# Opening products 512 columns wide, one token tile at a time, and softmax transposes moved inside the values' pass, in a two-layer float32 decoder trunk

## The chip, the cores and the metric

The kernel runs on one core of a Trainium2 chip. The metric is the device time of one execution in microseconds (us); the median over runs of the same program is compared.

## The reference

256 tokens of width 2048 go through two layers in float32. Layer 0 mixes tokens by causal pooling, layer 1 by dilated attention with three head groups; each layer ends in an MLP with squared ReLU, and every residual sum is layer-normed:

```
def strided_window_attention(q, k, v, dil, n_back, slopes): ...
    s = einsum(q, k) / sqrt(E) - slope * distance        # masked to the window
    p = softmax(s);  o = p @ v                           # and its log-sum-exp

def dilated_attention(x, w_qkv, w_out):
    qkv = (x @ w_qkv).reshape(B, S, 3, 3, 8, 128)        # type, group, slot
    merged = sum over groups of softmax(lse) * o
    return merged @ w_out                                # 1024 -> 2048

def sqrelu_mlp(x, w_up, w_down):
    h = relu(x @ w_up)                                   # 2048 -> 8192
    return (h * h) @ w_down

def reference(x, ...):
    for i in range(2):
        h = pool_mixer(x, ...) if i == 0 else dilated_attention(x, ...)
        x = layer_norm(ALPHA * x + h)
        x = layer_norm(ALPHA * x + sqrelu_mlp(x, ...))
```

## The kernel before, in words

Every float32 product is made of three products of rounded halves: an operand is split into a high part (a copy to the type float32r, on ACT, line 62) and a low part (the difference, on DVE, line 63), and high by high, low by high and high by low are summed in PSUM. Weights are streamed from HBM once, in chunks of 128 x 1024 numbers (512 KB). A chunk goes through three steps: a DMA into one of four `raw` tiles (line 125, issued by SP as soon as a tile is free), the copy `wh` on ACT and the difference `wl` on DVE into one of eight pairs of split tiles (`prefetch`, line 129). `weights()` hands out the next pair and first asks for the eight that follow; `resident(n)` hands out n at once, which stay in use until the last product that reads them. A `raw` tile is free when `wl` is done, a split pair when PE has done the products that read it. The order of work on PE, ACT and DVE is the order in which the code is written; each of these engines goes through its own list in order.

There are two forms of product. In `feature_major` (line 186) the weights are the stationary operand and the moving one is `xT`, the transposed x: per 128 rows of the weights and 128 columns, one matmul of 512 and one of 256. In `token_products` (line 239) 128 tokens of x are stationary and the weights move, 256 or 512 columns at a time, for each of two token tiles t. PSUM has eight banks, one tag with eight buffers, given out in rotation: a bank is written again eight allocations later, and waits until its readers are done.

A mixer or an MLP ends in `closing` (line 374), where the last 256 columns are made for token tile 0 first and then for tile 1, so that the norm of tile 0 runs beside tile 1's products. The normed tokens are transposed by PE (`ptr`, line 321), scaled on ACT (`xv`, line 330) and split on DVE into `xT` (lines 336 and 337). What follows a norm begins with `opening` (line 436): it takes the first 256 columns of the next weights, which are four chunks, does tile 0's products with all of them while tile 1 is still being normed (`normalise`, line 315), puts tile 1's transposes in, and then does tile 1's products with the same chunks. Line 447 asks for two more chunks before tile 1's products are issued. The norm's gain and bias are put on x itself later, in four `restore` steps (lines 352 and 353 on DVE, each two tiles of two operations), which `drain()` takes one at a time.

There are three openings: before the first MLP, before the attention, before the second MLP. In an MLP the opening's 256 columns go through `hidden` (ReLU `r` and square `q` on ACT, lines 531 and 533), then 256 columns and three times 512 columns follow feature-major; the opening's squares are transposed by PE (line 551) after the first of these. In the attention the opening makes the values of group 0 of the first pair of slots (`sp` 0); the values of the other two groups come in two passes of 256 columns (`project_value`). For later `sp` one pass of 512 columns makes two groups' values (`project_values`), and the softmax transposes (`transposes`, line 680) of the first slot stand behind it, followed by `values` (line 688), whose results go to bank `po`.

## Time and profile before

| | |
|---|---|
| median of 3 runs | 2147.08 us (2146.9 to 2147.69) |
| profiled execution: its time | 2146.52 us |
| profiled execution: its span | 2144.7 us |
| granted TensorE clock over the span | 0.999 |
| PE busy | 2124.7 us, 99% of the span |
| DVE busy | 1283.4 us, 60% |
| ACT busy | 1052.8 us, 49% |
| HBM read | 400.61 MB, 188 GB/s over the span |
| chain that ended last | PE 96%, DVE 2%, DMA 1%, ACT 1% |

The span runs from the first to the last instruction that the profiler recorded; the time of the execution has 1.8 us around it. Matmuls are pipelined: one 512 columns wide is shown as busy for some 390 ns, while the next starts after less, so distances between starts tell the rate. In the rows L62 is line 62, an arrow in brackets names what ended an engine's idle time, and a row with xN joins N instructions in a run.

### The profile page before, as it was taken

The numbers are of one execution on the slowest core, as the hardware profiler recorded it, in microseconds if no ns is written. First come the engines' busy times: TensorE is split into PE (matmuls) and PEld (weight loads), VectorE is DVE, ScalarE is ACT, GpSimd is POOL, SyncE is SP. The second block draws the span as 40 slices with busy tenths as digits, with TensorE's granted clock in tenths as the row PEclk, the third lists the DMA queues.
The fourth block names the chain that finished last, engine by engine and source line by source line (L and its number), as shares of the span: only waits on it lengthen the run. The fifth ranks groups of instructions, "written<-read, shape, count | busy, mean of one in ns | idle before, by whom it ended". The sixth has DMA issues, their size and how long they took to land.

```text
span 2144.7 us, 29773 instructions
## 1 busy us (share of the span) xinstructions
PE 2124.7 (99%) x11745; PEld 1845.9 (86%) x11745; DVE 1283.4 (60%) x1558; ACT 1052.8 (49%) x1368; POOL 23.0 (1%) x52
## 2 busy tenths in 40 slices
PE   8999999999999999999999999999999999999998
PEld 7889888888888888898998988888888888888887
DVE  6785756555455555578656565676655555554555
ACT  4563655454355355354545444455545534644541
POOL 1000000000000000001000000000000000000000
PEclk9999999999999999999999999999999999999999
DMA  7565567556655655548555555456665566566562
GB/s 239 204 216 177 169 204 237 175 199 201 191 185 196 194 172 206 194 139 237 173 175 161 176 162 173 164 164 218 209 221 178 201 197 188 176 207 186 181 207 94
DMA packets 256045, 404.67 MB, mean 189 GB/s; under 512 B 13104, under 2 KB 109984, under 8 KB 255648
## 3 DMA queue, kind: packets, MB, share of 16 engines
q1 hardware_dynamic: 253472, 394.31, 56.7%
q0 software_dynamic: 2432, 8.45, 1.9%
q8 instruction: 92, 1.51, 0.3%
q14 instruction: 49, 0.40, 0.1%
HBM read 400.61 MB, written 2.10 MB: 188 GB/s over the span
## 4 chain that ended last, share of the span: by engine, by line
PE 96%; DVE 2%; DMA 1%; ACT 1%; issue 0%; SPq 0%; DVEq 0%; ACTq 0%
PE pt L245 45%; PE pf L202 32%; PE pf L204 16%; PE pf L221 1%; PE pq L658 1%; PE po L697 1%; DMA raw<-in_attn_w_qkv 0%; DVE wl L63 0%; PE ptr L321 0%; DMA xz<-in_x 0%; ACT xv L330 0%; DVE xT L337 0%; DVE vL L63 0%; PE ptr L458 0%; DVE xT L336 0%
## 5 line engine op out<-in xcount | busy, mean ns | idle before, releaser
L63 DVE TENSOR_TENSOR wl<-raw,wh 128x1024 fp32r<-128x1024 f32 x744 | 898.2, 1224 | 621.1 <-ACT wh L62 607.1
L62 ACT ACTIVATE wh<-raw 128x1024 fp32r<-128x1024 f32 x744 | 773.4, 1057 | 805.8 <-PE pt L245 351.4
L202 PE MATMUL pf<-xT,wh 128*128 128x512 f32 x3008 | 947.6, 396 | 0.0
L204 PEld LDWEIGHTS pf<-xT,wl 128*128 128x128 f32 x3008 | 566.0, 188 | 134.0 <-DVE wl L63 0.6
L204 PE MATMUL pf<-xT,wl 128*128 128x256 f32 x3008 | 592.2, 278 | 0.0
L202 PEld LDWEIGHTS pf<-xT,wh 128*128 128x128 f32 x3008 | 459.5, 189 | 0.5
L245 PE MATMUL pt<-wl,hH 128*128 128x512 f32 (+1 forms) x1088 | 407.0, 377 | 0.0
L245 PE MATMUL pt<-wh,hH 128*128 128x512 f32 (+1 forms) x1088 | 407.0, 377 | 0.0
L245 PE MATMUL pt<-wh,hL 128*128 128x512 f32 (+1 forms) x1088 | 398.2, 377 | 0.0
L245 PEld LDWEIGHTS pt<-wl,hH 128*128 128x128 f32 x1088 | 204.8, 188 | 37.6 <-DVE wl L63 0.4
L245 PEld LDWEIGHTS pt<-wh,hH 128*128 128x128 f32 x1088 | 204.8, 188 | 37.5
L245 PEld LDWEIGHTS pt<-wh,hL 128*128 128x128 f32 x1088 | 199.6, 188 | 37.1
L245 PE MATMUL pt<-wh,xT 128*128 128x256 f32 (+1 forms) x704 | 156.4, 314 | 1.9 <-DVE xT L336 1.5
L245 PEld LDWEIGHTS pt<-wh,xT 128*128 128x128 f32 x704 | 117.2, 191 | 10.6 <-DVE xT L336 3.1
L63 DVE TENSOR_TENSOR hL<-q,hH 128x512 fp32r<-128x512 f32 x62 | 42.9, 693 | 125.6 <-ACT hH L62 125.6
L245 PE MATMUL pt<-wl,xT 128*128 128x256 f32 (+1 forms) x352 | 106.7, 312 | 0.0
L230 ACT ACTIVATE low<-pf 128x256 f32<-128x256 f32 x188 | 61.3, 377 | 69.6 <-PE pf L204 62.7
L245 PE MATMUL pt<-wh,pT 128*128 128x512 f32 (+1 forms) x320 | 82.6, 347 | 0.0
L231 DVE TENSOR_TENSOR u<-pf,low 128x256 f32<-128x256 f32 x172 | 64.7, 418 | 26.0 <-ACT low L230 26.0
L245 PEld LDWEIGHTS pt<-wl,xT 128*128 128x128 f32 x352 | 67.2, 191 | 3.6
L531 ACT ACTIVATE r<-u 128x512 f32<-128x512 f32 x62 | 39.2, 632 | 51.0 <-DVE u L231 51.0
L245 PEld LDWEIGHTS pt<-wh,pT 128*128 128x128 f32 x320 | 56.1, 189 | 7.5
(126 smaller groups left out, 1001.8 us busy)
## 6 DMA issues: line engine op xcount, KB each, us to landing
raw<-in_mlp_w_up SPq DMA_DIRECT2D x256, 512.0 KB, 4.4
raw<-in_mlp_w_down SPq DMA_DIRECT2D x256, 512.0 KB, 4.5
raw<-in_attn_w_qkv SPq DMA_DIRECT2D x120, 512.0 KB, 4.3
raw<-in_pool_w_in SPq DMA_DIRECT2D x32, 512.0 KB, 5.4
raw<-in_pool_w_out SPq DMA_DIRECT2D x32, 512.0 KB, 4.7
raw<-in_attn_w_qkv SPq DMA_DIRECT2D x48, 256.0 KB, 3.3
raw<-in_attn_w_out SPq DMA_DIRECT2D x16, 512.0 KB, 4.4
raw<-in_pool_w_group SPq DMA_DIRECT2D x8, 512.0 KB, 5.0
```

The source lines that it names most:

```text
L62: nc.scalar.activation(hi, src, AF.Copy)
L63: nc.vector.tensor_sub(lo, src, hi.bitcast(F32))
L202: nc.tensor.matmul(ps[b], hi[:, j, sl], a, start=(k == 0), stop=False, skip_group_check=True)
L204: nc.tensor.matmul(ps[b][:, 0, :], lo[:, j, sl], a[:, 0, :], start=False, stop=(k == nk - 1), skip_group_check=True)
L221: nc.tensor.matmul(ps[b // 2][:, b % 2, :], w[:, j, sl], a[:, part, :], start=(k == 0 and i == 0 and b % 2 == 0), stop=(k == nk - 1 and i ...
L230: nc.scalar.activation(low, p[:, 1, :], AF.Copy)
L231: nc.vector.tensor_add(out[:, b, :], p[:, 0, :], low)
L245: nc.tensor.matmul(ps, a[:, sl], u, start=(start and k == 0 and i == 0), stop=(k == nk - 1 and i == 2), skip_group_check=True)
L531: nc.scalar.activation(r, ps, AF.Relu)
L658: nc.tensor.matmul(pq[:, t, :], q[u][:, b, sl], k[v][:, b, :], start=(i == 0), stop=(i == 2))
L697: nc.tensor.matmul(po, v[:, st, b * P:(b + 1) * P], p[:, g, sl], start=(i == 0), stop=(i == 3 * 2 * GROUPS - 1))
```

## The change

The openings take 512 columns, eight chunks, instead of 256. Each token tile gets a PSUM bank of its own (before, both shared one), and the two chunks asked for ahead of tile 1's products are no longer asked for there. In an MLP the 256 columns that followed are part of the opening, and its squares need eight transposes instead of four. In the attention the opening makes the values of groups 0 and 1 of `sp` 0; group 2's follow by `project(2)`. The first slot's softmax transposes stand ahead of the last chunk of the values' pass for `sp` above 0, and behind the next `project(0)` for `sp` 0.

```diff
-UP_FIRST = (256, 256, 512, 512, 512)
 UP_REST = (512, 512, 512, 512)
-QKV_FIRST = ((2, 0), (0, 0), (1, 0), (0, 1), (1, 1), (0, 2), (1, 2), (2, 1), (2, 2))
-QKV_REST = QKV_FIRST[1:7] + ((2, 0),)
+QKV = ((0, 0), (1, 0), (0, 1), (1, 1), (0, 2), (1, 2))
...
-    def opening(norm, ncols):
-
-        both = bank([P, NT, ncols], "pt")
-        parts = resident(KT * ncols // CHUNK)
-        tile_products(both[:, 0, :], 0, KT, parts, x_parts,
+    def opening(norm):
+
+        ps = [bank([P, 512], "pt") for _ in range(NT)]
+        parts = resident(KT * 512 // CHUNK)
+        tile_products(ps[0], 0, KT, parts, x_parts,
                       between=[lambda: norm.transpose(1, 0), lambda: norm.transpose(1, 1)])
         for n in (2, 3):
             norm.transpose(1, n)
         for n in range(NG):
             norm.scaled(1, n)
             norm.features(1, n)
-        prefetch(state["used"] + 2)
-        tile_products(both[:, 1, :], 1, KT, parts, x_parts, start=False)
+        tile_products(ps[1], 1, KT, parts, x_parts)
         pending.extend(norm.restores())
-        return both
+        return ps
...
-                q0 = hidden(opening(norm_in, UP_FIRST[0])) if c == 0 else None
-                for ncols in UP_FIRST[1:] if c == 0 else UP_REST:
+                q0 = [hidden(p.rearrange("p (b n) -> p b n", b=2)) for p in opening(norm_in)] if c == 0 else None
+                for ncols in UP_REST[1:] if c == 0 else UP_REST:
                     ps = feature_major(KT, ncols, x_act)
                     if q0 is not None:
...
-        def project_values():
-            ps = token_major(KT, 512, x_parts)
+        def value_halves(ps):
             hi, lo = value_pair()
             for t in range(NT):
                 split_from(hi[:, t], lo[:, t], ps[t].rearrange("p (g n) -> p g n", g=2))
             drain()
             return [(hi[:, :, i], lo[:, :, i]) for i in range(2)]
...
             if sp == 0:
-                vs.append(halves(2, opening(norm1, 256)))
+                vs.extend(value_halves(opening(norm1)))
...
-            if sp == 0:
-                pair = value_pair()
-                vs.append(project_value(pair, 0))
-            else:
-                vs.append(project(2))
+            vs.append(project(2))
...
-            vs.extend([project_value(pair, 1)] if sp == 0 else project_values())
-            transposes(sc[js[0]])
+            if sp == 0:
+                later.append(lambda sc=sc, js=js: transposes(sc[js[0]]))
+            else:
+                vs.extend(value_halves(token_major(KT, 512, x_parts, before_last=lambda: transposes(sc[js[0]]))))
```

How the lists of three engines change. ACT, from tile 1's scaling in the first MLP's opening to the first transposed squares (`xv` scales, `r` and `q` are ReLU and square, `wh` weight copies, `hH` the copy of the squares); before:

```order
L330 ACTIVATE xv<-ptr,cols 128x128 x24
L62 ACTIVATE wh<-raw 128x1024 x2
L531 ACTIVATE r<-pt 128x512
L533 ACTIVATE q<-r 128x512
L62 ACTIVATE wh<-raw 128x1024 x9
L62 ACTIVATE hH<-ptr 128x512
```

and with the change:

```order
L330 ACTIVATE xv<-ptr,cols 128x128 x8
L60 ACTIVATE wh<-raw 128x1024 x4
L330 ACTIVATE xv<-ptr,cols 128x128 x16
L531 ACTIVATE r<-pt 128x512
L533 ACTIVATE q<-r 128x512
L531 ACTIVATE r<-pt 128x512
L533 ACTIVATE q<-r 128x512
L60 ACTIVATE wh<-raw 128x1024 x15
L60 ACTIVATE hH<-ptr 128x512 x2
```

Four copies, of the opening's own second half, now stand ahead of tile 1's scaling; the two copies of the next weights that stood ahead of `r` are behind the second `q`.

DVE, from the end of tile 1's split to the first projection's joined result `u` in the attention (`vL` is the low part of the values, L352 and L353 a `restore`); before:

```order
L337 TENSOR_TENSOR xT<-xv,xT 128x4x128
L63 TENSOR_TENSOR wl<-raw,wh 128x1024 x2
L63 TENSOR_TENSOR vL<-pt,vH 128x512
L63 TENSOR_TENSOR wl<-raw,wh 128x1024 x9
L231 TENSOR_TENSOR u<-pf,low 128x256 x2
```

and with the change:

```order
L337 TENSOR_TENSOR xT<-xv,xT 128x4x128
L61 TENSOR_TENSOR vL<-pt,vH 128x512 x2
L352 TENSOR_TENSOR xz<-xz,gb 128x512
L353 TENSOR_TENSOR xz<-xz,gb 128x512
L352 TENSOR_TENSOR xz<-xz,gb 128x512
L353 TENSOR_TENSOR xz<-xz,gb 128x512
L61 TENSOR_TENSOR wl<-raw,wh 128x1024 x11
L231 TENSOR_TENSOR u<-pf,low 128x256 x2
```

The values' low parts and a whole `restore` stand ahead of all differences of the next weights.

PE, the first MLP, where the transposes of the opening's squares end and the next feature-major pass begins, with the waits that each instruction carries (numbers tell tiles apart; `pf_2557` to `pf_2560` and `pf_2414` to `pf_2417` are that pass's four banks); before:

```order
L551 MATMUL ptr_2383<-ident_94,q_2261 128x128 x3
L202 MATMUL pf_2414<-xT_110,wh_2279 128x512 [waits Activation_49]
L202 MATMUL pf_2415<-xT_110,wh_2279 128x512
L204 MATMUL pf_2414<-xT_110,wl_2280 128x256 [waits DVE_49]
L204 MATMUL pf_2415<-xT_110,wl_2280 128x256
L202 MATMUL pf_2416<-xT_110,wh_2279 128x512
L202 MATMUL pf_2417<-xT_110,wh_2279 128x512
```

and with the change:

```order
L552 MATMUL ptr_2511<-ident_94,q_2278 128x128
L202 MATMUL pf_2557<-xT_110,wh_2350 128x512 [waits Activation_49]
L202 MATMUL pf_2558<-xT_110,wh_2350 128x512 [waits PE_49]
L204 MATMUL pf_2557<-xT_110,wl_2351 128x256 [waits DVE_49]
L204 MATMUL pf_2558<-xT_110,wl_2351 128x256
L202 MATMUL pf_2559<-xT_110,wh_2350 128x512 [waits DVE_49]
L202 MATMUL pf_2560<-xT_110,wh_2350 128x512 [waits DVE_49]
```

The third and fourth bank of the pass now carry a wait for DVE of their own.

## Rows read from the trace of the kernel before

**Rows 1.** The page, part 1: busy time, share of the span, instructions by engine.

```profile
PE 2124.7 (99%) x11745; PEld 1845.9 (86%) x11745; DVE 1283.4 (60%) x1558; ACT 1052.8 (49%) x1368; POOL 23.0 (1%) x52
```

**Rows 2.** The chain that ended last, in order of time: start, length, what.

```profile
221.08 0.87 PE ptr L321 x8
...
485.00 87.05 PE pt L245 x384
...
1011.91 11.52 PE pt L245 x96
```

**Rows 3.** Timeline of PE, first MLP's opening: start, length, instruction, shape, count.

```profile
215.63 0.36 PE L245 MATMUL pt<-wh,xT 128*128 128x256 f32 x1
...
229.86 0.63 PE L202 MATMUL pf<-xT,wh 128*128 128x512 f32 x2
230.33 0.39 PE L204 MATMUL pf<-xT,wl 128*128 128x256 f32 x2
...
241.01 0.60 PE L551 MATMUL ptr<-ident,q 128*128 128x128 f32 x4
```

**Rows 4.** Timeline of DVE, the same stretch.

```profile
221.95 1.00 DVE L315 TENSOR_SCALAR xz<-xz,mv,r 128x512 f32<-128x512 f32 x2
...
232.37 2.36 DVE L63 TENSOR_TENSOR wl<-raw,wh 128x1024 fp32r<-128x1024 f32 x2 [1.61 <-ACT wh L62]
...
247.52 0.68 DVE L63 TENSOR_TENSOR hL<-ptr,hH 128x512 fp32r<-128x512 f32 x1
248.12 0.75 DVE L231 TENSOR_TENSOR u<-pf,low 128x256 f32<-128x256 f32 x2
```

**Rows 5.** Timeline of PE, the attention's opening.

```profile
927.25 0.36 PE L245 MATMUL pt<-wh,xT 128*128 128x256 f32 x1
...
941.49 0.63 PE L202 MATMUL pf<-xT,wh 128*128 128x512 f32 x2
```

**Rows 6.** Timeline of DVE, the attention's opening and first projections.

```profile
933.57 1.00 DVE L315 TENSOR_SCALAR xz<-xz,mv,r 128x512 f32<-128x512 f32 x2
...
960.50 0.68 DVE L352 TENSOR_TENSOR xz<-xz,gb 128x512 f32<-128x512 f32 x1
...
974.70 0.69 DVE L63 TENSOR_TENSOR qkL<-u,qkH 128x512 fp32r<-128x512 f32 x1 [0.70 <-ACT qkH L62]
```

**Rows 7.** Timeline of PE, the second MLP's opening.

```profile
1423.49 0.36 PE L245 MATMUL pt<-wh,xT 128*128 128x256 f32 x1
...
1438.49 0.63 PE L202 MATMUL pf<-xT,wh 128*128 128x512 f32 x2
```

**Rows 8.** Timeline of DVE, the second MLP's opening.

```profile
1430.58 1.00 DVE L315 TENSOR_SCALAR xz<-xz,mv,r 128x512 f32<-128x512 f32 x2
```

**Rows 9.** Timeline of ACT, first MLP, from tile 1's products on.

```profile
230.12 0.60 ACT L531 ACTIVATE r<-pt 128x512 f32<-128x512 f32 x1 [0.93 <-PE pt L245]
...
231.29 1.99 ACT L62 ACTIVATE wh<-raw 128x1024 fp32r<-128x1024 f32 x2
234.08 1.06 ACT L62 ACTIVATE wh<-raw 128x1024 fp32r<-128x1024 f32 x1 [0.81 <-DMA raw<-in_mlp_w_up]
...
241.17 1.06 ACT L62 ACTIVATE wh<-raw 128x1024 fp32r<-128x1024 f32 x1 [0.94 <-DMA raw<-in_mlp_w_up]
...
246.25 0.58 ACT L62 ACTIVATE hH<-ptr 128x512 fp32r<-128x512 f32 x1
```

**Rows 10.** Timeline of PE, end of the values' pass for `sp` 1, and behind `values`.

```profile
1147.02 0.27 PE L683 MATMUL pp<-ident,sc 128*128 128x128 f32 x1
...
1151.07 0.27 PE L683 MATMUL pp<-ident,sc 128*128 128x128 f32 x1
```

**Rows 11.** The chain that ended last, in order of time: the first matmuls of the program, and later ones.

```profile
8.78 0.85 PE pf L202 x2
...
15.40 0.47 PE pf L202 x2
```

**Rows 12.** Stretch 10 to 12 us: length, busy of PE, PEld, DVE, ACT, POOL, granted clock, DMA share, GB/s.

```profile
10.00:12.00 2.00, 2.00 (x8) 1.71 (x8) 1.36 (x2) 0.45 (x1) 0.00 (x0) 1.00 1.05 375
```

More of the change, by code (lines that the diff above doesn't have):

```diff
@@ L87, in plan_mlp @@
         for c in range(MLP_PARTS):
-            plan_columns(w_up[l], 0, KT, c * D, UP_FIRST if c == 0 else UP_REST)
+            plan_columns(w_up[l], 0, KT, c * D, UP_REST)
             plan_columns(w_down[l], c * KT, KT, 0, CLOSING if c == MLP_PARTS - 1 else UP_REST)
@@ L92, in qkv_col, with plan_values @@
         return ty * GROUPS * GW + g * GW + sp * 256
-    def plan_values(sp):
+    def plan_values(sp, g):
         w_v = w_qkv.rearrange("p k (y g n) -> p k y g n", y=3, g=GROUPS)
         for k in range(0, KT, 2):
-            chunks.append((w_v[:, k:k + 2, 2, 1:3, sp * 256:(sp + 1) * 256], 2, 512))
+            chunks.append((w_v[:, k:k + 2, 2, g:g + 2, sp * 256:(sp + 1) * 256], 2, 512))
     plan_columns(w_in, 0, KT, 0, UP_REST)
@@ L105, in trunk @@
     for sp in range(SLOTS // 2):
-        for ty, g in QKV_FIRST if sp == 0 else QKV_REST:
+        if sp == 0:
+            plan_values(sp, 0)
+        for ty, g in QKV + ((2, 2 if sp == 0 else 0),):
             plan(w_qkv, 0, KT, qkv_col(sp, ty, g), 256)
         if sp > 0:
-            plan_values(sp)
+            plan_values(sp, 1)
     plan_columns(w_merge, 0, SLOTS, 0, CLOSING)
@@ L543, in mlp @@
                 hs = []
-                q0 = hidden(opening(norm_in, UP_FIRST[0])) if c == 0 else None
-                for ncols in UP_FIRST[1:] if c == 0 else UP_REST:
+                q0 = [hidden(p.rearrange("p (b n) -> p b n", b=2)) for p in opening(norm_in)] if c == 0 else None
+                for ncols in UP_REST[1:] if c == 0 else UP_REST:
                     ps = feature_major(KT, ncols, x_act)
                     if q0 is not None:
-                        pt = bank([P, 2, S], "ptr")
-                        for b in range(2):
-                            for t in range(NT):
-                                nc.tensor.transpose(pt[:, b, t * P:(t + 1) * P], q0[:, t, b * P:(b + 1) * P], ident)
-                        hs.append(split_hidden(pt))
+                        for b0 in range(0, 4, 2):
+                            pt = bank([P, 2, S], "ptr")
+                            for b in range(2):
+                                for t in range(NT):
+                                    nc.tensor.transpose(pt[:, b, t * P:(t + 1) * P],
+                                                        q0[t][:, b0 // 2, b * P:(b + 1) * P], ident)
+                            hs.append(split_hidden(pt))
                         q0 = None
@@ L632, in project_values @@
             return [(hi[:, :, i], lo[:, :, i]) for i in range(2)]
-        def project_value(pair, i):
-            hi, lo = (v[:, :, i] for v in pair)
-            split_from(hi, lo, token_major(KT, 256, x_parts, shared=True))
-            drain()
-            return hi, lo
         def project(ty):
@@ L736, in trunk @@
                 weigh(sc[j], m)
-            vs.extend([project_value(pair, 1)] if sp == 0 else project_values())
-            transposes(sc[js[0]])
+            if sp == 0:
+                later.append(lambda sc=sc, js=js: transposes(sc[js[0]]))
+            else:
+                vs.extend(value_halves(token_major(KT, 512, x_parts, before_last=lambda: transposes(sc[js[0]]))))
             def first(sc=sc, vs=vs, js=js):
```

## The prediction

> **What bounds the kernel now.** Read the page's busy shares first: PE is busy 99% of the span [rows 1]. Whatever shortens its work or makes it wait shows in full, and no other engine is near. The chain of waits gives the rates. A run of 96 token-major matmuls, 256 columns wide, lasts 11.52 us, 120 ns each; 384 of 512 columns last 87.05 us, 227 ns each; eight transposes last 0.87 us [rows 2]. Then read the timelines of the three openings, where PE has little work and the other engines much. In the first MLP the opening lasts from 215.63 to 229.86, 14.23 us [rows 3]; its 96 matmuls and 16 transposes need 11.52 + 1.74 us, so PE waits 0.97 us there. In the attention it is 14.24 us [rows 5], a wait of 0.98; in the second MLP 15.00 us [rows 7], a wait of 1.74. All other waits of PE are small, so the change can gain little, and the question is what it adds.
>
> **PE's own work.** In an MLP the opening and the pass of 256 columns behind it (229.86 to 241.01, 11.15 us [rows 3]) are 22.67 us. They become 96 matmuls of 512 columns, 21.76 us, and four more transposes, 0.44 us: 0.47 us less. In the attention three times 11.52 us become 21.76 + 11.52: 1.28 us less. Sum: **-2.2 us**. In the trace two matmuls of 256 columns cost 13 ns more than one of 512 [rows 2]. [...]
>
> **Tile 0's products wait for their own weights.** The opening now needs eight chunks. Four are split as before; the other four need the buffers that `closing` holds, and stand behind the norm's work on DVE (the order of ACT shows the same four ahead of the last 16 `xv`). Tile 0 starts when it does now, and uses a chunk in six matmuls of 227 ns, 1.36 us. After four chunks and the first matmul of the fifth, 5.67 us, it needs the fifth `wl`. DVE is through with `normalise` at 221.95 + 1.00 = 222.95 and needs 1.23 us for the difference (a third row shows two back to back in 2.36) [rows 4]: 224.18, while PE asks at 215.63 + 5.67 = 221.30. That is a wait of 2.9 us. In the attention: 933.57 + 1.00 + 1.23 = 935.80 [rows 6] against 932.92, 2.9 us. In the second MLP: 1430.58 + 2.23 = 1432.81 [rows 8] against 1429.16, 3.65 us. The later three chunks come faster than they are used (1.23 against 1.36 us), and tile 1's transposes and scaling fit behind them. These 9.45 us replace the 3.69 us of waits above: **+5.8 us**.
>
> **Behind tile 1's products nothing is ready.** Call T the moment when PE could start the next pass. Before, two chunks were split by then; now none, since ACT must first do the squares of tile 1, which end with tile 1's last matmul. ACT's rows give the delay: `r` starts 0.26 us after T (230.12 against 229.86), and after `r`, `q` and the first copy of the pair at 231.29 [rows 9] the difference starts at 232.37 and takes 1.2 us [rows 4]: the low part is there at T + 3.75, where PE wants it 0.47 us after T (230.33 [rows 3]). PE waits 3.3 us in each MLP, in two pieces. In the attention DVE has a low part of the values and then a `restore` ahead of the first difference (the order of DVE): the copy of tile 1's values ends at T + 0.85, like `r`; then 0.69 us for `vL` (as the `qkL` row, same shape), four operations of 0.68 us [rows 6], and 1.23: T + 5.45, a wait of 5.0 us. Queued behind it on DVE are all ten further differences, but those then come faster than PE uses them, a chunk in 2.79 us (11.15 us by four [rows 3]). Sum: **+11.6 us**.
>
> **A bank that isn't free.** In the MLP, counted from the first of the four banks of the pass behind the opening, allocations 5 and 6 are now the two tiles of transposed squares, so the next pass gets 7, 8, 1 and 2, and 1 and 2 still hold the pass before. That is the wait for DVE that `pf_2559` and `pf_2560` carry and their forerunners don't. Their readers, `u`, stand on DVE behind 15 differences and two `hL`. The 15th is bound by the four `raw` tiles: a tile comes round in 7.1 us (234.08 to 241.17, four copies on [rows 9]). The third difference is done at T + 6.2, three rounds later it is T + 27.5; two `hL` (0.68 each) and two `u` (0.75 together) [rows 4] end at T + 29.6. PE has done the pass at T + 3.3 + 22.3, eight transposes and a first half step (0.70 us) at T + 27.2, and asks for the second of the banks 0.23 us later: a wait of 2.2 us, twice: **+4.4 us**. Its ends: 1.6 us if the refill were no limit (the transposes, two `hH` of 0.58 us [rows 9], `hL` and `u` alone), 4.3 us if a round took a tenth longer.
>
> **The first scores.** Before, `qkL` of the first keys ends at 975.39 [rows 6], 33.9 us after the opening, when PE needs it. In that stretch DVE now has two differences, a `vL` and a `restore` more, 2.46 + 0.69 + 2.72 = 5.9 us, while PE comes 5.0 us later: **+0.8 us**, between 0 (DVE has some idle time there) and 2.4.
>
> **The values' passes.** From the first transpose at 1147.02 to the first one behind `values` at 1151.07 [rows 10] are 4.05 us, of which nine transposes (0.98) and 18 matmuls of 256 columns (2.16) are work and 0.9 us is waiting. With the transposes ahead of the last chunk their splits end beside it, but the values' own splits still end some 1.5 us after the pass, while group 0 covers 0.72 us. I take half the wait as gone: 0.5 us in each of three passes, **-1.5 us**, between 0 and -2.7. For `sp` 0 the transposes move behind a projection, where softmax is long done: nothing. The other edits cost nothing: the loads are the same bytes, and ACT and DVE have the rest of each 2.79 us free.
>
> **Sum.** -2.2 + 5.8 + 11.6 + 4.4 + 0.8 - 1.5 = +18.9 us. Against the profiled execution's own 2146.52 us this is 2165.4 us; the median of the runs lies 0.56 us above that execution, so I say 2166 us.
>
> **The rivals.**
> - *PE slows after its new waits.* The first matmuls of the program follow a wait for the input: the chain has 0.85 us for a pair of 512 columns at 8.78 us, and 0.47 us at 15.40 [rows 11]. [...] Half rate from 8.4 to 12.7 us loses about 2.1 us. If each of the eight new waits of over 2 us (three in tile 0, three behind tile 1, two for banks) brought that, it is +17 us: 2183 us. Against it: inside or just before each wait PE has work, where the start had none. [...] Chance 0.12.
> - *No bank conflict.* If the banks were not given out in rotation, or the readers were done, the fifth term is gone: 2161.5 us. The wait in the order of PE speaks against it. Chance 0.08.
> - *The next weights aren't late* (the other side). If ACT got to the next copies beside tile 1's products, where it and DVE idle for some 6 us, and to the opening's second half before tile 0 asks, the second, third and fourth terms go, and -2.2 - 1.5 us remain: 2143.4 us. The point that decides is whether a copy can start before tile 1's last matmul has ended. Against it: in the rows `r` has ACT waiting 0.93 us for PE although the next `raw` tiles are loaded, and the copies come behind it [rows 9]. If only part of this held, the time would be within 0.2% of before. Chance 0.08.
>
> **How the numbers follow.** The forecast keeps 0.72. Its own ends are -2.2 + 5.8 + 11.6 + 3.2 + 0 - 2.7 = +15.7 and -2.2 + 5.8 + 11.6 + 8.6 + 2.4 + 0 = +26.2, that is 2162.8 and 2173.3 us. The range reaches to the case without a conflict, to waits half a us shorter than worked out at each place, and on the other side to a slow clock at about two of the eight places: 2158 to 2177 us. A measurement of this kernel tells 0.2%, 4.3 us, from no change. All cases but the last are slower by more: 0.92. The last is split: 0.05 within 0.2%, 0.03 faster.
>
> **What would show it.** In the profile of the changed kernel: a wait of PE for `wl` of about 3 us in the middle of tile 0's products, three times; ACT's `wh` directly behind the second `q`, and PE starting the next pass 2.5 us late and waiting again for `wl`; in the attention about 5 us there; about 2 us before the third bank of the second feature-major pass, with DVE's `u` as what ended it; the token-major rate of 227 ns in the openings. The prediction is wrong if PE's idle time in an opening grows by less than 3 us, or if the matmuls after the waits are spaced like the program's first ones.

## The result, and the profile after

The changed kernel takes **2174.22 us** (median of 4 runs, 2172.88 to 2175.55) against 2147.39 us (4 runs, 2146.9 to 2148.23) before: a ratio of 1.0125, 95% interval 1.0107 to 1.0142. It is slower by 26.8 us. The forecast was 2166 us, its range 2158 to 2177 us. The profiled execution of the changed kernel took 2175.18 us, its span is 2173.4 us: 28.7 us more than the one before.

The page, part 1 and the first line of part 4, after: PE has 10.5 us more of busy time than in [rows 1] with 216 matmuls less, and of the chain PE now has 92% instead of 96%, DVE 4% instead of 2%.

```profile
PE 2135.2 (98%) x11529; PEld 1841.9 (85%) x11529; DVE 1281.0 (59%) x1554; ACT 1050.8 (48%) x1364; POOL 23.1 (1%) x52
...
PE 92%; DVE 4%; DMA 2%; ACT 1%; issue 1%; SPq 0%; DVEq 0%; ACTq 0%
```

The waits of PE after: line, tile, releaser, us in total, times, longest. The waits for `wl`, `wh` and `hL` come to 20.5 us; the same list of the kernel before has none of these five groups; its entry for the openings is the last line here.

```profile
PE pt L245 <- DVE wl L61: 7.6, 3, 2.5
PE pf L202 <- ACT wh L60: 6.2, 3, 2.3
...
PE pf L204 <- DVE wl L61: 3.4, 2, 2.8
PE pf L202 <- DVE hL L61: 2.8, 2, 2.4
...
PE pt L245 <- ACT wh L60: 0.5, 1, 0.5
PE pq L653 <- DVE qkL L61: 0.3, 1, 0.3
```

```profile
PE pt L245 <- DVE xT L336: 1.5, 3, 1.0
```

The timeline of PE in the first MLP after, from the opening on, answers to [rows 3]. The fifth `wl` comes 2.52 us late. Tile 1's products end at 245.23 - 2.29 = 242.94; there PE waits for the first high part, then for the first low part. At 272.59 it waits for a bank, and what ended that wait is `hL`.

```profile
216.23 0.48 PE L245 MATMUL pt<-wh,xT 128*128 128x512 f32 x1
...
224.73 0.50 PE L245 MATMUL pt<-wl,xT 128*128 128x512 f32 x1 [2.52 <-DVE wl L61]
...
245.23 0.73 PE L202 MATMUL pf<-xT,wh 128*128 128x512 f32 x2 [2.29 <-ACT wh L60]
...
246.49 0.50 PE L204 MATMUL pf<-xT,wl 128*128 128x256 f32 x2 [0.52 <-DVE wl L61]
...
272.59 0.49 PE L202 MATMUL pf<-xT,wh 128*128 128x512 f32 x1 [2.43 <-DVE hL L61]
```

ACT at the same place answers to [rows 9]: `r`, `q`, and only then the copies.

```profile
242.98 0.60 ACT L531 ACTIVATE r<-pt 128x512 f32<-128x512 f32 x1 [6.71 <-PE pt L245]
243.61 0.63 ACT L533 ACTIVATE q<-r 128x512 f32<-128x512 f32 x1
244.14 1.99 ACT L60 ACTIVATE wh<-raw 128x1024 fp32r<-128x1024 f32 x2
```

DVE answers to [rows 4]: the last normalising of tile 1, the opening's second four differences behind it, those of the next pass behind tile 1's products, and much later the `u` of that pass.

```profile
222.54 1.00 DVE L315 TENSOR_SCALAR xz<-xz,mv,r 128x512 f32<-128x512 f32 x2
223.46 4.62 DVE L61 TENSOR_TENSOR wl<-raw,wh 128x1024 fp32r<-128x1024 f32 x4
...
245.21 4.63 DVE L61 TENSOR_TENSOR wl<-raw,wh 128x1024 fp32r<-128x1024 f32 x4 [8.92 <-ACT wh L60]
...
273.05 0.74 DVE L231 TENSOR_TENSOR u<-pf,low 128x256 f32<-128x256 f32 x2
```

Those waits are as forecast. What the sum had left out stands in the granted clock. Windows of the changed kernel (stretch, length, busy time and count of PE, PEld, DVE, ACT, POOL, granted clock, DMA share, GB/s), each behind a new wait: the first MLP's two, the attention's two, the second MLP's two.

```profile
224.00:228.00 4.00, 3.27 (x14) 2.74 (x15) 4.00 (x4) 0.49 (x1) 0.00 (x0) 1.00 0.54 154
246.00:250.00 4.00, 3.51 (x20) 3.11 (x21) 3.84 (x4) 2.03 (x3) 0.00 (x0) 1.00 0.60 176
944.00:948.00 4.00, 3.91 (x10) 3.10 (x11) 3.44 (x4) 0.00 (x0) 0.00 (x0) 0.57 0.64 166
968.00:976.00 8.00, 6.90 (x24) 5.98 (x25) 4.45 (x4) 0.32 (x1) 1.09 (x2) 0.57 0.70 183
1450.00:1456.00 6.00, 5.66 (x13) 4.46 (x14) 3.69 (x4) 0.08 (x1) 0.00 (x0) 0.50 0.74 231
1474.00:1480.00 6.00, 5.96 (x18) 4.57 (x18) 4.80 (x5) 3.43 (x4) 0.00 (x0) 0.50 0.66 217
```

In four of these six places the granted clock fell: to 0.57 over both windows of the attention, to 0.50 over both of the second MLP. In tile 0 the waits were of one length (2.52 us in the first MLP, where it did not fall; 2.53 and 2.54 where it did), and behind tile 1's products the two MLPs waited 2.29 us each, of which one fell; only the attention waited longer there (1.63 and 2.83 us). Busy time by the missing share of the clock gives an estimate of 3.91 x 0.43 + 6.90 x 0.43 + 5.66 x 0.50 + 5.96 x 0.50 = **10.5 us** lost. The chain shows it in the same 17 matmuls of the three openings (first MLP, attention, second MLP):

```profile
224.73 4.15 PE pt L245 x17
...
944.09 5.75 PE pt L245 x17
...
1450.34 6.89 PE pt L245 x17
```

### The profile page after: what moved, and what is told of

Its sections match the earlier page's. It is cut to its first block, busy times and chain, and to the rows that moved or that the text cites. A ratio compares the mean times of both kernels' runs of the same rounds, so it can differ in the third digit from the quotient of the medians.

```text
span 2173.4 us, 29327 instructions
## 1 busy us (share of the span) xinstructions
PE 2135.2 (98%) x11529; PEld 1841.9 (85%) x11529; DVE 1281.0 (59%) x1554; ACT 1050.8 (48%) x1364; POOL 23.1 (1%) x52
## 4 chain that ended last, share of the span: by engine, by line
PE 92%; DVE 4%; DMA 2%; ACT 1%; issue 1%; SPq 0%; DVEq 0%; ACTq 0%
PE pt L245 45%; PE pf L202 30%; PE pf L204 15%; DVE wl L61 1%; PE pq L653 1%; DMA raw<-in_mlp_w_up 1%; PE po L692 1%; DMA raw<-in_attn_w_qkv 1%; ACT wh L60 1%; PE ptr L321 0%; DVE xT L337 0%; PE pf L221 0%; DMA raw<-in_pool_w_group 0%; DVE win L498 0%; DMA xz<-in_x 0%
## 5 line engine op out<-in xcount | busy, mean ns | idle before, releaser
L202 PE MATMUL pf<-xT,wh 128*128 128x512 f32 x2944 | 932.1, 398 | 9.2 <-ACT wh L60 6.2
L204 PEld LDWEIGHTS pf<-xT,wl 128*128 128x128 f32 x2944 | 556.0, 189 | 136.8 <-DVE wl L61 5.6
L204 PE MATMUL pf<-xT,wl 128*128 128x256 f32 x2944 | 581.9, 279 | 3.4 <-DVE wl L61 3.4
L202 PEld LDWEIGHTS pf<-xT,wh 128*128 128x128 f32 x2944 | 452.0, 190 | 12.0 <-ACT wh L60 7.5
L245 PE MATMUL pt<-wh,xT 128*128 128x512 f32 (+1 forms) x640 | 172.1, 354 | 0.5 <-ACT wh L60 0.5
L245 PE MATMUL pt<-wl,xT 128*128 128x512 f32 (+1 forms) x320 | 113.4, 354 | 7.6 <-DVE wl L61 7.6
L245 PEld LDWEIGHTS pt<-wl,xT 128*128 128x128 f32 x320 | 61.9, 193 | 15.9 <-DVE wl L61 8.5
```

The source lines that it names most:

```text
L202: nc.tensor.matmul(ps[b], hi[:, j, sl], a, start=(k == 0), stop=False, skip_group_check=True)
L204: nc.tensor.matmul(ps[b][:, 0, :], lo[:, j, sl], a[:, 0, :], start=False, stop=(k == nk - 1), skip_group_check=True)
L245: nc.tensor.matmul(ps, a[:, sl], u, start=(start and k == 0 and i == 0), stop=(k == nk - 1 and i == 2), skip_group_check=True)
```

## The experiments

Each time is compared with the kernel before on the same chip. Edits are shown against the changed kernel where nothing else is said. The table gives, for the profiled execution of each version, by how much three stretches are longer than before, counted from the first matmul of one stage to the first of another (us), and in how many places ahead of the program's end the granted clock fell. It holds one profiled execution of each version; experiment 2 shows that the loads from HBM alone can move an MLP's entry by some 2 us:

```
version                        first MLP      from there to       second MLP     clock
                               opening to     the attention's     opening to     falls
                               down products  merge               down products
the change                        +8.0            +8.9               +11.1         4
copies first                      +2.5            -1.2                +4.2         1
filled waits                      +5.9            +9.1                +6.9         1
squares inside                    +8.0           +11.1                +6.6         6
two ahead                         +9.6            +8.3                +8.2         4
values' passes only                0.0            -1.0                 0.0         0
late restore                      +8.9            +4.6                +8.9         6
splits first                      +5.9            +6.1                +5.1         2
both orders                       +0.9            -2.9                +0.9         0
deviation late                    +1.6            -2.0                +1.8         0
mixed                             +7.8            -2.0                +8.1         2
attention only                     0.0            -1.6                 0.0         0
```

**1. Copies first.** The next pass's chunks are split behind tile 1's products in program order, ahead of the squares or the values.

```diff
         tile_products(ps[1], 1, KT, parts, x_parts)
+        prefetch(state["used"] + 7)
         pending.extend(norm.restores())
```

> The changed kernel with one line more: seven of the next chunks are asked for right behind tile 1's products, so that their copies and differences stand ahead of the squares (in the attention ahead of the values' splits and the restore). Theory (work in order behind tile 1): PE's waits for the first copy and difference go, 3.2 us in each MLP and 5.0 in the attention, and with them the half clock that follows two of them (2.6 and 3.2 us); the bank wait shrinks by 1 to 2 us because the refill starts earlier. 2174 - 11.4 - 5.8 - 1.5 = about 2155.5 us. Rival (the refill by DMA is the limit): the copies come earlier, but PE runs out of chunks a few us later, and the time falls by less than 6 us, to 2168 or more.

Measured: 2152.62 us (10 runs, 2150.72 to 2154.72), ratio 1.0023 (1.0014 to 1.0032). The waits of PE for weights and banks that are left:

```profile
PE pt L245 <- DVE wl L61: 7.6, 3, 2.5
...
PE pf L202 <- DVE hL L61: 0.6, 2, 0.3
PE pt L245 <- ACT wh L60: 0.5, 1, 0.5
```

The whole term behind tile 1's products is gone, and with it most of the bank's wait; the waits in tile 0 stand untouched. So 21.6 of the 26.8 us came back, and most of them hung on one thing: that the next pass's copies stood behind the squares or the values of tile 1. Forecast for this term were 11.6 us, and 4.4 for the bank. The rest is the slow clock: an estimated 6.0 us of it stood behind tile 1's products in the change, where no wait is left now. The edit does not touch the waits in tile 0, yet behind them the clock fell once here (0.52 from 1434 to 1436 us) and twice in the change, so part of the gain, some 3 us in the profiled executions, is chance.

**2. Filled waits.** The changed kernel with matmuls that nobody reads where PE waits: ten in the middle of tile 0's products, ten (in the attention nineteen) around the first low part of the next pass. They add work and take none away.

```diff
+    def fill(dst, n):
+        for _ in range(n):
+            nc.tensor.matmul(dst, xT[:, 0, 0, :P], xT[:, 0:4, 0, :P], start=True, stop=True, skip_group_check=True)
...
         for i, (hi, lo) in enumerate(parts):
+            if i == len(parts) // 2 and filled is not None:
+                fill(filled, 10)
```

> The changed kernel with matmuls added that nobody reads, where PE waits in the openings: ten of 512 columns ahead of the fifth chunk of tile 0, and in the first pass behind the opening nine and one (MLP) or seven and twelve (attention) ahead of the first and behind the first two matmuls. They leave all waits for ACT and DVE in place and add work. Theory (the clock falls because PE idles): the granted clock stays at 1.00 in all openings and the 10 us that the profile lost at half clock in the attention's and the second MLP's openings come back, 2174 to about 2164 us, with PE's idle time there under 1 us each. Rival (the slow matmuls have another cause, such as the DMA traffic or the operands just written): the slow stretches stay and the time is 2174 us or a little more.

Measured: 2170.13 us (4 runs, 2168.38 to 2171.83), ratio 1.0104 (1.0089 to 1.0119): 4.1 us faster than the change, though PE does more. No clock fell in any opening (1.00 in every stretch of 2 us from 210 to 270, 930 to 990 and 1430 to 1490 us), which is what the theory says and its rival denies. One fall is left (0.50 from 1002 to 1004 us), at a wait that the filling did not cover, the first scores:

```profile
PE pq L664 <- ACT qkH L60: 2.3, 1, 2.3
```

The second MLP got 4.2 us shorter (11.1 to 6.9). In the attention the gain went to this new wait and the fall behind it: in the change PE comes there later, and the scores' operands are ready. So the clock is a cost of its own beside the waits, as the first theory said, but it is not a sum of losses that can all be had back: part of what PE lost to the slow clock it would have waited for DVE anyway (2.3 us for the first scores here, none in the change). The expected 10 us were too many by 6.

The first MLP got 2.1 us shorter as well, and there the clock stood at 1.00 in both executions. This gain is the bank's wait, 0.29 us instead of 2.43, and it comes from the loads. In the change ACT waited 4.26 us for the load of the pass's fifth chunk, here 2.05; so the fifteenth difference ended 1.8 us after PE asked for the bank in the change (270.70 + 1.23 against 272.59 - 2.43), and 0.6 us before it here (267.49 + 1.22 against 269.56 - 0.29). ACT and DVE in the change, then ACT, DVE and PE in this run:

```profile
252.29 1.06 ACT L60 ACTIVATE wh<-raw 128x1024 fp32r<-128x1024 f32 x1 [4.26 <-DMA raw<-in_mlp_w_up]
270.70 1.23 DVE L61 TENSOR_TENSOR wl<-raw,wh 128x1024 fp32r<-128x1024 f32 x1 [0.59 <-ACT wh L60]
...
249.18 1.06 ACT L60 ACTIVATE wh<-raw 128x1024 fp32r<-128x1024 f32 x1 [2.05 <-DMA raw<-in_mlp_w_up]
267.49 1.22 DVE L61 TENSOR_TENSOR wl<-raw,wh 128x1024 fp32r<-128x1024 f32 x1 [0.47 <-ACT wh L60]
269.56 1.09 PE L205 MATMUL pf<-xT,wh 128*128 128x512 f32 x2 [0.29 <-DVE hL L61]
```

**3. Squares inside.** The transposes of the opening's squares and their splits stand in the middle of the pass instead of behind it.

```diff
-                    ps = feature_major(KT, ncols, x_act)
-                    if q0 is not None:
+                    def squares(q0=q0):
                         for b0 in range(0, 4, 2):
                             pt = bank([P, 2, S], "ptr")
...
-                        q0 = None
+                    ps = feature_major(KT, ncols, x_act, inside=squares if q0 is not None else None)
+                    q0 = None
```

> The changed kernel with the transposes and splits of the opening's squares moved into the middle of the feature-major pass behind it. Theory (the wait behind that pass is for the banks of the transposed squares, whose readers stand behind 15 differences): the wait of 2.4 us in the first MLP and 0.4 us in the second go, 2174 to about 2171 us. Rival (it is the pass's own banks, read by u): the readers u still stand behind the differences, the wait stays at 2 us or so, and the time does not move.

Measured: 2173.62 us (4 runs, 2172.21 to 2175.53), ratio 1.0121 (1.0106 to 1.0136): not to be told from the change. The wait for `hL` (2.8 us in all) is out of PE's list, so it was the transposed squares' banks. The 2171 us expected with it did not come: this execution's clock fell in six places (to 0.50 to 0.54 in the lowest 2 us of each), the first MLP's two among them, and that stage kept its length. In the attention PE waits 2.0 us for the first scores. The time alone would speak for the rival; the list of waits speaks against it.

**4. Two ahead.** Two of the opening's second four chunks are split earlier in the closing, ahead of tile 0's last features, and all four normalisings of tile 1 come later.

```diff
         norm.features(0, 2)
-        norm.normalise(1, 0)
-        norm.normalise(1, 1)
+        prefetch(state["used"] + 6)
         norm.features(0, 3)
-        norm.normalise(1, 2)
-        norm.normalise(1, 3)
+        for n in range(NG):
+            norm.normalise(1, n)
```

> The changed kernel with two of the opening's four late chunks split ahead of the normalising of tile 1 instead of behind all of it. Theory (PE in tile 0 waits for DVE's order): the fifth difference is ready some 1.6 us earlier, the three waits of 2.5 to 3.2 us fall to about 1.3, and the half clock behind two of them (1.6 and 2.7 us) goes: 2174 - 4.8 - 4.3 = about 2165 us. Rival (tile 1's norm is then late instead): PE waits as much longer for tile 1's split or for the seventh chunk, and the time falls by less than 3 us.

Measured: 2172.77 us (4 runs, 2172.29 to 2173.42), ratio 1.0116 (1.0099 to 1.0132). The wait for own weights came in six pieces instead of three, 1.1 us longer in all:

```profile
PE pt L245 <- DVE wl L61: 8.7, 6, 2.2
```

The time missed the theory's 2165 us and the rival held as written: PE now waits for the fifth chunk (0.8 us) and again for the seventh (2.2 us). That leaves open whether DVE has too much work by then or only the wrong order. The timeline of DVE in this run (first MLP) speaks for the order: the last two differences stand behind 1.91 us of normalising that no one needs yet.

```profile
221.90 2.36 DVE L61 TENSOR_TENSOR wl<-raw,wh 128x1024 fp32r<-128x1024 f32 x2 [1.03 <-ACT wh L60]
224.63 0.69 DVE L337 TENSOR_TENSOR xT<-xv,xT 128x512 fp32r<-128x512 f32 x1
225.24 1.91 DVE L315 TENSOR_SCALAR xz<-xz,mv,r 128x512 f32<-128x512 f32 x4
227.06 2.35 DVE L61 TENSOR_TENSOR wl<-raw,wh 128x1024 fp32r<-128x1024 f32 x2
```

**5. Splits first.** So all four differences go ahead of tile 1's normalising, and behind tile 0's last features.

```diff
         norm.features(0, 2)
-        norm.normalise(1, 0)
-        norm.normalise(1, 1)
         norm.features(0, 3)
-        norm.normalise(1, 2)
-        norm.normalise(1, 3)
+        prefetch(state["used"] + 8)
+        for n in range(NG):
+            norm.normalise(1, n)
```

> The changed kernel with the splits of the opening's second four weight chunks ahead of the normalising of token tile 1 on VectorE (2 us of it stood ahead of them), nothing else. If the wait for tile 0's own weights is VectorE's order, not its sum of work, the three waits of 2.5 us shrink to 0.5 to 0.9 us each: 5.0 us less, and the two stretches at half clock behind them (4.3 us in the profiled execution) go as well: about 2165 us, 2162 to 2169.5. Rival (VectorE's sum of work binds, as the run that drew two chunks ahead suggests): the waits stay at 7 us or more in all, 2172 or above.

Measured: 2163.13 us (5 runs, 2162.09 to 2164.85), ratio 1.0076 (1.0064 to 1.0089): 11.1 us faster than the change. The waits of PE:

```profile
PE pf L202 <- ACT wh L60: 6.2, 3, 2.3
...
PE pf L204 <- DVE wl L61: 3.9, 3, 2.8
PE pt L245 <- DVE wl L61: 2.6, 3, 0.9
PE pf L202 <- DVE hL L61: 1.5, 2, 1.1
```

Tile 0's waits fell from 7.6 to 2.6 us and no clock fell there; behind tile 1's products, where the waits are unchanged, it still fell in two of three places (granted clock over the span 0.996, against 0.993 in the change). It was DVE's order, not its work.

**6. Late restore.** One `restore` of the normed x is not done behind the split values of the attention's opening, but later.

```diff
-        def value_halves(ps):
+        def value_halves(ps, restore=True):
...
-            drain()
+            if restore:
+                drain()
...
-                vs.extend(value_halves(opening(norm1)))
+                vs.extend(value_halves(opening(norm1), restore=False))
```

> The changed kernel without the one restore (four passes of VectorE over half the columns' x, 2.7 us) that stands behind the split values of the opening, ahead of the next weights' low parts; it is done at a later place instead. The attention's wait behind tile 1's products falls from 4.95 to about 2.3 us, as in the MLPs: 2174.2 minus 2.7 = 2171.5 us, and about 2169 if the stretch at half clock behind it (2.6 us lost) goes too. Rival: the restore meets another wait later, or ScalarE's high parts set the wait alone; then 2173 to 2174.5.

Measured: 2168.69 us (4 runs, 2168.17 to 2169.62), ratio 1.0102 (1.0088 to 1.0115). The wait fell as the theory had it. The clock fell behind it all the same, so the reason given for the lower of the two expected times did not hold, though the time did. In the profiled execution the matmuls stayed slow for less time than in the change: steps of four start 1.27 to 1.28 us apart, instead of 0.70, from 968.72 to 971.27 us here and from 969.70 to 974.82 us there; the second MLP was 2.2 us shorter too. PE in the attention, behind tile 1's products, in this run:

```profile
966.41 0.73 PE L202 MATMUL pf<-xT,wh 128*128 128x512 f32 x2 [1.63 <-ACT wh L60]
967.66 0.50 PE L204 MATMUL pf<-xT,wl 128*128 128x256 f32 x2 [0.52 <-DVE wl L61]
```

In the changed kernel the second of these waits was 2.83 us:

```profile
965.53 0.73 PE L202 MATMUL pf<-xT,wh 128*128 128x512 f32 x2 [1.63 <-ACT wh L60]
...
969.10 0.80 PE L204 MATMUL pf<-xT,wl 128*128 128x256 f32 x2 [2.83 <-DVE wl L61]
```

The same run shows how little the clock's fall is the program's. Up to the attention it is the changed kernel, with the same waits in the first MLP; there the change kept 1.00 in its windows, and here the clock fell behind both:

```profile
224.00:228.00 4.00, 3.16 (x8) 2.50 (x9) 4.00 (x4) 0.59 (x1) 0.00 (x0) 0.57 0.51 155
...
248.00:252.00 4.00, 3.91 (x14) 3.33 (x15) 3.44 (x4) 1.62 (x2) 0.00 (x0) 0.57 0.71 210
```

Yet this stage is only 0.9 us longer than in the change (8.9 against 8.0): the bank's wait shrank from 2.43 us to 0.3, in part because PE came later, in part because the loads came sooner, as in experiment 2.

**7. Values' passes only.** The kernel before with the softmax transposes inside the values' pass of the later slot pairs, and nothing else.

```diff
-        def project_values():
-            ps = token_major(KT, 512, x_parts)
+        def project_values(inside):
+            ps = token_major(KT, 512, x_parts, before_last=inside)
...
-            vs.extend([project_value(pair, 1)] if sp == 0 else project_values())
-            transposes(sc[js[0]])
+            if sp == 0:
+                vs.append(project_value(pair, 1))
+                transposes(sc[js[0]])
+            else:
+                vs.extend(project_values(lambda: transposes(sc[js[0]])))
```

> The kernel before with one part of the change alone: the softmax transposes stand inside the values' pass of the later slot pairs (three passes); the openings keep 256 columns. If the landmarks of the changed kernel are right, each such pass saves 0.4 us of the lag, 1.2 us in all: 2146.2 us against 2147.4 before, and the step from the attention's opening to its merge is 1.2 us shorter. My forecast's own 0.5 us a pass would give 2145.9. Rival: the lag shrinks only because the openings shift the stages against each other; then 2147.4 and no difference that can be measured.

Measured: 2145.82 us (11 runs, 2145.04 to 2146.69) against 2147.18, ratio 0.9993 (0.9985 to 1.0002). The medians differ by 1.4 us, the interval takes in no difference; the profiled execution has the three passes 1.2 us shorter in all, the same as in the changed kernel (from the first matmul of the pass to that of the next stage 26.3 us instead of 26.7, three times).

**8. Both orders.** Experiments 1 and 5 in one kernel.

> The changed kernel with both orders: the opening's second four chunks are split ahead of tile 1's normalising, and the next pass's seven chunks behind tile 1's products, ahead of the squares or the split values. Terms left against the kernel before: tensor work -2.2, values' passes -1.2, own weights 2.0 instead of the old 3.6 us of waits at the same place, bank 0.6: about 2145.5 us, 2143.5 to 2148, faster than both kernels or level with the one before. Rival (the waits of tile 0 stay): 2152 or above.

Measured: 2145.54 us (11 runs, 2144.84 to 2146.65), ratio 0.9993 (0.9984 to 1.0002): 28.7 us faster than the change, and level with the kernel before; that it is faster is not shown. No clock fell in an opening (over the span it reads 0.999, as before). DVE in the first MLP's opening: the differences first, then the normalising. PE's list of waits has none for the normalising, and 0.9 us for the opening's own weights in each opening, as in experiment 5.

```profile
221.38 4.63 DVE L61 TENSOR_TENSOR wl<-raw,wh 128x1024 fp32r<-128x1024 f32 x4
225.92 1.91 DVE L315 TENSOR_SCALAR xz<-xz,mv,r 128x512 f32<-128x512 f32 x4
```

**9. Deviation late.** Experiment 8 with tile 1's standard deviation behind these splits too.

```diff
-        norm.rstd(1)
         norm.features(0, 2)
         norm.features(0, 3)
         prefetch(state["used"] + 8)
+        norm.rstd(1)
```

> The version with both orders, and token tile 1's standard deviation too (five small passes on VectorE, 0.9 us, one on ScalarE) behind the splits of the opening's second four chunks. If VectorE's place in line still sets the 0.9 us that each opening waits for its own weights, the three waits fall from 2.6 us to about 0.6 in all: 2145.5 minus 2.0 = 2143.5 us, faster than both kernels. Rival (tile 1's transposes now come late, or the high parts on ScalarE bind): 2145 to 2146.5.

Measured: 2147.88 us (11 runs, 2147.04 to 2148.75), ratio 1.0004 (0.9995 to 1.0013). The expectation fell, and the time lies above the rival's 2146.5 us too. Both of the rival's reasons are in the profile: the wait for own weights is the 2.6 us that it was, since the features of tile 0 now wait for ACT, and tile 1's transposes wait as well.

```profile
PE pt L245 <- DVE wl L61: 2.6, 3, 0.9
PE ptr L321 <- DVE xz L315: 1.7, 3, 0.6
```

**10. Mixed.** Experiment 9 with 256 columns in the MLPs' openings again (edit against experiment 9).

```diff
+UP_FIRST = (256, 256, 512, 512, 512)
...
-                q0 = [hidden(p.rearrange("p (b n) -> p b n", b=2)) for p in opening(norm_in)] if c == 0 else None
+                q0 = hidden(opening_shared(norm_in, UP_FIRST[0])) if c == 0 else None
```

> The version before this one with the two MLPs' openings at 256 columns again, as in the kernel before; only the attention keeps 512. The wider opening saves 0.47 us of tensor work in an MLP and waits about 0.2 us more for own weights and 0.3 for a bank: near nothing either way, 2143.5 us, 2142.5 to 2144.5. If the MLPs' wide openings were still a loss (0.85 us each with both orders), 2141.8; if they were a gain by then, 2144.5.

Measured: 2159.98 us (5 runs, 2159.12 to 2162.3), ratio 1.0063 (1.005 to 1.0075), far from every value expected. Tile 0's products are half as long at 256 columns, and the late normalising can't hide behind them: three waits of PE, the longest of 6.3 us, and a fall of the clock in each of the two MLPs' openings (over the span it reads 0.995; in the first MLP matmuls of 256 columns start 0.21 us apart behind the wait of 6.3 us, 0.12 ahead of it).

```profile
PE ptr L322 <- DVE xz L316: 13.2, 3, 6.3
```

**11. Attention only.** The wide opening and the two orders of experiment 8 at the attention alone; the MLPs' openings and the closings ahead of them as before. The edit is shown against experiment 9; `wide` is set for the closings of the MLPs, one of which stands ahead of the attention.

```diff
+        norm.rstd(1)
         norm.features(0, 2)
-        norm.features(0, 3)
-        prefetch(state["used"] + 8)
-        norm.rstd(1)
-        for n in range(NG):
+        if wide:
+            norm.features(0, 3)
+            prefetch(state["used"] + 8)
+        else:
+            norm.normalise(1, 0)
+            norm.normalise(1, 1)
+            norm.features(0, 3)
+        for n in range(0 if wide else 2, NG):
             norm.normalise(1, n)
```

> The wide opening and both new orders at the attention alone; the two MLPs and the closings ahead of them are as in the kernel before (256 columns, tile 1's normalising ahead of the splits). By landmarks of the run with both orders the attention is then 2.64 us shorter than before (9.74 minus 12.38, the three values' passes among it) and each MLP gives back 0.85 to 0.91: about 2147.0 minus 2.6 = 2144.4 us, faster than both kernels and than the version with both orders. If the late normalising was not what cost the version before it 13 us, about 2155 or above.

Measured: **2144.09 us** (11 runs, 2142.98 to 2144.42) against 2147.05, ratio 0.9984 (0.9975 to 0.9993): the one version that is faster than both kernels beyond its interval, by 3 us. It also settles where the run before it lost its time: with the old order ahead of the MLPs, both MLPs are as long as before.

## Why the prediction was right, and what its sum lacked

The direction, the place of each wait and the cause of all but one came out as worked out; 2174.2 us lies in the range, 8 us above the forecast. By its own terms, in the profiled execution:

- *PE's own work, -2.2 us.* Tile 1's products keep 227 ns a matmul, and the openings hold 21.76 + 1.74 us of work as said. No run here measures the term alone.
- *Own weights, +5.8.* From the opening's start to T are 242.94 - 216.23 = 26.7 us in the first MLP, 3.2 us more than its work (forecast 2.9); by the same reckoning, less the slow clock, it is an estimated 3.1 us in the attention and 3.9 in the second MLP (forecast 2.9 and 3.65), which without the 3.69 us of before makes 6.5. DVE's normalising ends where it was said to, and the difference behind it lets PE go. Experiment 5 shows that the order on DVE made this wait.
- *Behind tile 1's products, +11.6.* In the first MLP the first low part's matmuls start at 246.49, 3.1 us after T + 0.47 (forecast 3.3); in the attention T is 965.53 - 1.63 = 963.90 and they start at 969.10, 4.7 us late (forecast 5.0); with 3.1 us in the second MLP the term measured 10.9. Experiments 1 and 6 show both parts of it: the copies behind `r` and `q`, and the restore.
- *A bank that isn't free, +4.4.* 2.43 us in the first MLP (forecast 2.2), but 0.35 in the second, so 2.8. There the last difference came 1.6 us sooner after T (1497.48 + 1.23 against T = 1471.30), which leaves an estimated 0.9 us of the wait; only the last half us is owed to the slow clock, by which PE came later. The cause was **misnamed**: the forecast, like the description of the kernel, had the banks given out in plain rotation, with `u` as the reader that holds them. The row has `hL`, and PE goes on at 272.59, before DVE begins with `u` at 273.05; experiment 3, which only moves the transposed squares, takes the wait away. So the pass gets the squares' own banks.
- *First scores, +0.8.* 0.3 us in the change, where the slow clock ahead of them had made PE late; 2.0 and 2.3 us, and 0.3 behind that, in executions where the clock stayed low for less time ahead of them (experiment 3: 0.51 and 0.63 from 968 to 972 us, where the change has 0.53, 0.50, 0.50 and 0.76 from 968 to 976) or not at all (experiment 2: 1.00), near the upper end of 2.4 that the forecast gave. The high part that PE needs is ready 41 to 42 us after T in all three; PE comes some 41.3, 39.9 and 39.4 us after it.
- *Values' passes, -1.5.* -1.2 us in three passes, alone as well as in the change.

What failed is the step "the forecast keeps 0.72" with its sum free of any clock: the loss to the slow clock was a rival, all or nothing, at a chance of 0.12, with 2.1 us at each of eight places. It came on top of the forecast's own terms, at four places, with 1.7 to 3.0 us each: an estimated 10.5 us. With PE's own work taken as forecast, the terms as measured come to -2.2 + 6.5 + 10.9 + 2.8 + 0.3 - 1.2 = 17.1 us instead of 18.9; with the clock that is 27.6 of the 28.7 us by which the profiled execution is longer. The argument against it, that PE has work inside and just before each wait, did not hold: a wait of 2.5 us in the middle of steady products was enough in two of three places. Behind it experiment 2 stands, in which the waits filled with matmuls brought no fall in any opening.

One of the two signs that the prediction named for being wrong came true in part: behind four of the waits the matmuls are spaced like the program's first ones, as the 6.89 us for 17 of them against 4.15 show. Behind these waits the granted clock reads 0.50 to 0.57; in the stretch of [rows 12] it shows no fall, so no run shows that the two have one cause. That the time lies in the range all the same is partly luck. The range had room for a slow clock at two places, 4.2 us by the prediction's own price; it came at four and took 10.5 us.

Why the clock falls in one execution and not in another stays open: in the first MLP the late restore has the change's code and the same waits, and the windows behind them read 0.57 there and 1.00 in the change.

The rival on the other side (copies that find their place beside tile 1's products) was true of the machine but not of this program: experiment 1 puts them there with one line.

## What to carry to other kernels

A wider first product needs its weights earlier by as much as it is wider; before widening it, follow the engines that prepare these weights and ask what stands ahead of them that nobody needs yet. Moving one call gave back most of the loss here, and the order that suits one width cost 6 us an opening at another. Where PE is busy 99% of the time, price a new wait of a few microseconds with the clock that may fall behind it (an estimated 1.7 to 3.0 us a place here), as a cost added to the wait with a chance at each place, and not as one case for all places at once.

## What the runs showed of the hardware that was not expected

- Behind waits of PE of about 2 to 2.8 us the granted clock fell in some places and some executions and not in others: in the changed kernel behind the waits of 2.53 and 2.54 us in tile 0 (0.57 and 0.50 over the windows above) but not behind that of 2.52 (1.00). With copies first, the three waits of 2.5 us brought one fall. With both orders, where no wait in an opening is longer than 0.9 us, there was none. What decides between two waits of the same length is open.
- A slow stretch was not always lost: where PE would next have waited for DVE, the later wait was shorter instead (the high part for the first scores: 2.3 us without a slow stretch ahead of it, none in the change). A shorter wait is no proof of it: the bank's was 2.43 us in one execution and 0.29 in another, both at a granted clock of 1.00, because the loads came sooner.
- In the first MLP ACT stood idle for 6.71 us and DVE for 8.92 us beside tile 1's products (rows above), though the next chunks were loaded: with copies first ACT copies four of them there without a wait. Engines that are busy for 48% and 59% of the span were the bottleneck for the few microseconds that counted.
